# One recorded list of 2,598 steps sets the order of all five engines of a transformer-block kernel

## The chip, the cores and the metric

The kernel runs on one core of a Trainium2 chip. A core has five engines with a queue of instructions each: TensorE (PE, matrix products), VectorE (DVE), ScalarE (ACT), GpSimd (POOL) and SyncE (SP, which here only starts DMA transfers). The metric is the device time of one execution in microseconds (us), lower being better. Times come from the hardware: a median of several runs, and one profiled execution that leaves a trace of every instruction.

## The reference

One decoder layer on 512 tokens of width 1024, in float32, cut to what matters:

```python
h = x
h = h + 0.5 * swiglu(rmsnorm(h, ffn1_norm), ffn1_w_gate, ffn1_w_up, ffn1_w_down)      # width 2816
proj = rmsnorm(h, mix_norm) @ w_in
u, v, z, xbc, dt_raw = split(proj)
ya = chunked_spatial_gating(gelu(u), gelu(v), ln_g, ln_b, w_s, b_s)    # chunks of 128 tokens, causal
ya = rmsnorm(ya, gm_out_norm)
yb = mamba2_mixer(z, xbc, dt_raw, ...)     # convolution of 4 taps, 16 heads of 64, state 128, chunks of 128
h = h + concat([ya, yb]) @ w_out
h = h + 0.5 * swiglu(rmsnorm(h, ffn2_norm), ffn2_w_gate, ffn2_w_up, ffn2_w_down)
gate = sigmoid(rmsnorm(h, ple_norm) @ ple_w_gate + ple_b_gate)
h = h + gate * (p @ ple_w_proj)
return rmsnorm(h, final_norm)
```

## The kernel before

**Tiling.** Activations lie feature-major: `h` is eight tiles of 128 features x 512 tokens. Weights come in blocks of 128 x 1024 (512 KB) through the three buffers of `raw` and the like. Every block is split into two parts that the fast matmul format holds exactly: ScalarE casts the high part (`whi`, lines 185 and 421), VectorE subtracts it and leaves the low part (`wlo`, lines 186 and 422). A product then is three passes (lines 215 to 217, or 598 in the feed-forward blocks): high by high, low by high, high by low. Eight row blocks by three passes are 24 matmuls. The feed-forward blocks save products by a scheme in which seven sums of blocks are multiplied in place of eight; some of its sums are made by DMAs that GpSimd issues and that add while they load (lines 613, 616, 650).

**Stages.** (1) The embedding product `p @ ple_w_proj` in two halves (`embedding`, line 843), put into DRAM; (2) the first feed-forward block; (3) the mixer: the `w_in` products, convolution (959), step sizes and running sums, chunk states (1072; GpSimd's multiply at 1069, TensorE's products at 1076), two heads at a time the attention-like part (`decayed` 1095, `ssd` 1115), gating (`gated` 1138), the spatial gating (`mix` 1279); (4) `w_out` and the second feed-forward block; (5) the gate with the embedding (`gate` 1380), in the last three feature tiles by token halves (`gate_half` 1424), the final norm's sums (`factors` 1434) and the output tiles (`rows_out` 1445).

**Norms.** The mean square of a token is needed over features, which lie across partitions: ScalarE squares, VectorE or GpSimd adds up (267), TensorE multiplies by ones (276), VectorE finds the reciprocal root in small Newton steps (233 to 238), and a product with a diagonal spreads it to all partitions (`sm` at 306, kept as `rall` at 312). Products begin on unnormed data, and the factor is put in afterwards.

**What sets the order.** In stages (1), (2) and (4), `run` (line 348) issues steps by hand on PE, ACT, DVE and SP: loads 6 steps ahead, splits two ahead, what follows a product behind the next one. GpSimd is not in that order. The mixer and stage (5) are written as plain code, and the framework's scheduler orders them. A tile gets its buffer where the code asks for it. Of the eight PSUM banks three are for `mm`, two for `acc`, three for `sm`, each group in turn.

Of the kernel before, what the change touches and what calls it, by code (L numbers as in the profile page):

```python
# [42 lines left out]
AHEAD = 5  # L43
WARM = 10
BY_HALF = 3
LOADS = 6
# [3 lines left out]
    "nv": 2, "ny": 2, "nt": 2, "bnst": 2, "rlast": 2,  # L50
    "F": 1, "xfa": 2, "xfb": 2, "x": 16, "xs": 8, "u": 8, "emb": 8, "raw0": 1, "embt": 1, "rawb": 3,
# [30 lines left out]

@with_exitstack
def layer_kernel(ctx: ExitStack, tc: tile.TileContext, a: dict, out: bass.AP):
    nc = tc.nc
    PSUM = bass.MemoryType.PSUM
    base = ctx.enter_context(tc.tile_pool(name="sb", bufs=1))

    region = {"left": None, "right": None}
    names = {}  # L90
    count = [0]

    def pad(pool, name):
# [12 lines left out]
    def open_region(side, name):
        close_region(side)
        names[side] = name
        region[side] = tc.alloc_tile_pool(name=name, bufs=1, side=side, reuse_waits="tile")
        if side == "left":  # L110
            pad(region[side], name)

    psum = ctx.enter_context(tc.tile_pool(name="ps", bufs=1, space=PSUM))
    dram = ctx.enter_context(tc.tile_pool(name="dr", bufs=1, space=bass.MemoryType.DRAM))

    def sb(tag, shape=(P, T), dt=F32):
        count[0] += 1
        pool = region[REGION[tag]] if tag in REGION else base
        return pool.tile(list(shape), dt, tag=tag, bufs=BUFS.get(tag, 1), name=f"{tag}_{count[0]}")
# [4 lines left out]
    def bank(tag, n):  # L124
        count[0] += 1
        return psum.tile([P, T], F32, tag=tag, bufs=n, name=f"{tag}_{count[0]}")

    turns = {"mm": 0, "rawb": 0}

    def mm_ps():  # L130

        turns["mm"] += 1
        return bank("acc", 2) if turns["mm"] % 5 in (2, 4) else bank("mm", 3)

    def sm_ps():
        return bank("sm", 3)
# [25 lines left out]
    nc.scalar.copy(vec_warm, ones[:, 0:1])  # L162

    upper = sb("upper", (P, P))
    nc.gpsimd.affine_select(
        out=upper, in_=ones, pattern=[[1, P]], compare_op=ALU.is_ge, fill=0.0, base=0,
        channel_multiplier=-1,
    )
# [81 lines left out]
    class Norm:  # L250
# [18 lines left out]
        def sums(self):  # L269
# [4 lines left out]
            ps = sm_ps()  # L274
# [40 lines left out]
        @classmethod  # L315
        def on_all(cls, tok):
# [31 lines left out]
    def run(steps, opened=None):  # L348
# [8 lines left out]

        for i in range(LOADS):
            do(i, "load")
        for i in range(-3, n + 2):  # L360
# [7 lines left out]
            if i == opened:  # L368
                open_region("right", "ffn2_right")
                for k in held:  # L370
                    do(k, "load")
            late = 0 <= i - 1 < n and not steps[i - 1].urgent
            if 0 <= i - 2 < n and len(steps[i - 2].after) > 1:
                steps[i - 2].after[1]()
            for what in ("split", "after") if late else ("after", "split"):
# [460 lines left out]
    emb_dram = dram.tile([P, ND, T], F32, name="emb_dram", tag="emb_dram")  # L836
# [6 lines left out]
    def embedding(q):  # L843
# [46 lines left out]
    pad(base, "sb")  # L890
    x_ffn1, x_mix = [], []

    norm = Norm(nc.vector)
    steps, mix_norm = swiglu(
        "ffn1", x_ffn1, norm, lambda: open_region("left", "mix_left"),
# [11 lines left out]
    def squares(*ds):  # L907
        for d in ds:
            norm.add(h[d])
# [6 lines left out]
    for k, i in ((4, 3), (6, 2), (9, 4), (10, 1)):  # L916
# [7 lines left out]
    with tc.manual_schedule(engines=ORDERED):  # L924
        run(steps)
    norm = mix_norm
    open_region("right", "mix_right")


    x = x_mix  # L930
    w_in = a["w_in"]

    def project(unit, w=None):
        w = w or weights(w_in[unit], D)
        ps = mm_ps()
        accumulate(ps, w, 0, x)
        return ps
# [3 lines left out]
    w_dt = Unit(w_in[0], D)  # L941
    w_dt.load(0, D)
    nc.scalar.copy(w_dt.hi, w_dt.raw)
    both = w_dt.hi.rearrange("p (k m) -> p k m", k=ND)
    nc.vector.tensor_tensor(
        both[:, :, HEADS : 2 * HEADS],
        w_dt.raw.rearrange("p (k m) -> p k m", k=ND)[:, :, :HEADS],
        both[:, :, :HEADS].bitcast(F32), ALU.subtract,
    )
    ps = mm_ps()  # L950
    for n, k in enumerate(D_ORDER):
        for i in range(2):
            nc.tensor.matmul(
                ps, both[:, k, :], x[k][i], start=n + i == 0, stop=n + i == ND
            )
    dt_raw = tmp()
    nc.vector.tensor_copy(dt_raw[: 2 * HEADS], ps[: 2 * HEADS])

    def conv(ps, i, tag):
        raw = sb("convin", (P, T + 3))  # L960
        nc.vector.memset(raw[:, 0:3], 0.0)
        nc.vector.tensor_tensor(raw[:, 3:], ps, r, ALU.mult)
        o = sb(tag)
        nc.scalar.activation(
            o, raw[:, 0:T], AF.Identity, scale=col("conv_w", 4 * i), bias=col("conv_b", i)
        )
        for j in range(1, 4):
            nc.vector.scalar_tensor_tensor(
                o, raw[:, j : j + T], col("conv_w", 4 * i + j), o, ALU.mult, ALU.add
            )  # L970
        nc.scalar.activation(o, o, AF.Silu)
        return o
# [4 lines left out]
    early = [project(1)]  # L977
    rtok = norm.per_token(D)
    early.append(project(2))
    r = norm.on_all(rtok)  # L980
    bc = [conv(ps, 8 + i, "ya") for i, ps in enumerate(early)]
    dt_ps = sm_ps()
    for c in range(NC):
        nc.tensor.transpose(
            dt_ps[:, 2 * c * HEADS : 2 * (c + 1) * HEADS],
            dt_raw[: 2 * HEADS, c * P : (c + 1) * P], ident[: 2 * HEADS, : 2 * HEADS],
        )
    dtb = vec[:, _COL["dt_bias"] : _COL["dt_bias"] + HEADS]
    neg_a = sb("nega", (P, HEADS))
    nc.scalar.activation(neg_a, vec[:, _COL["a_log"] : _COL["a_log"] + HEADS], AF.Exp)  # L990
    nc.vector.tensor_scalar(neg_a, neg_a, -1.0, None, ALU.mult)
# [566 lines left out]
```

## Time and profile before

| | us |
|---|---|
| median of three runs | 1110.29 |
| lowest and highest of them | 1108.97, 1111.76 |
| span of the profiled execution | 1109.7 |
| TensorE busy in it | 1085.0 (98%) |
| VectorE | 781.7 (70%) |
| ScalarE | 513.8 (46%) |
| GpSimd | 132.0 (12%) |

The trace is read in this order: the page's busy times, then stretches of the span (busy time of each engine, the granted TensorE clock as a share of 2.4 GHz, the DMA engines' busy share), then what TensorE waited for, then timelines of single places. A busy TensorE is not TensorE at its peak, since matmuls overlap and their ends are modelled.

### The profile page before, as it was taken

How to read it: one execution, taken by the hardware profiler on the slowest of the kernel's cores; microseconds unless marked ns; L12 is line 12 of the kernel's file. 1: busy time of each engine (PE TensorE's matmuls, PEld its weight loads, DVE VectorE, ACT ScalarE, POOL GpSimd, SP SyncE). 2: the span in 40 equal slices, each digit the busy share in tenths (PEclk: the TensorE clock that was granted, in tenths of full speed). 3: DMA queues.
4: the chain of work that ended last, by engine and by line, in shares of the span. 5: the costliest groups of instructions: out<-in, count | busy, mean ns of one | idle time of the engine just before them, and what ended most of it. 6: DMA issues, size and time to landing. Idle time of an engine off the chain costs nothing.

```text
span 1109.7 us, 16404 instructions
## 1 busy us (share of the span) xinstructions
PE 1085.0 (98%) x6631; PEld 954.1 (86%) x6631; DVE 781.7 (70%) x1071; ACT 513.8 (46%) x709; POOL 132.0 (12%) x124
## 2 busy tenths in 40 slices
PE   9889999999999999999999999999999999999997
PEld 6779999999998787777888888889999999999887
DVE  5887776766667688576776664868767767667766
ACT  6545444444345374656443343544444443434554
POOL 2000000000001201244200000000000000000311
PEclk9999999999999999999999999999999999999998
DMA  9667757566631323234523233477677666643412
GB/s 353 201 164 202 198 153 190 163 188 155 184 95 57 96 79 107 95 112 133 160 78 96 76 95 114 146 175 194 188 190 189 177 185 174 163 123 110 138 54 76
DMA packets 49036, 161.66 MB, mean 146 GB/s; under 512 B 5568, under 2 KB 5824, under 8 KB 48960
## 3 DMA queue, kind: packets, MB, share of 16 engines
q1 hardware_dynamic: 34128, 117.46, 31.0%
q0 software_dynamic: 9232, 33.56, 16.7%
q10 hardware_dynamic: 5600, 9.60, 2.8%
q8 instruction: 52, 0.85, 0.3%
q14 instruction: 24, 0.20, 0.1%
HBM read 156.33 MB, written 4.26 MB: 145 GB/s over the span
## 4 chain that ended last, share of the span: by engine, by line
PE 83%; DVE 9%; ACT 4%; issue 2%; POOL 1%; DMA 1%; SPq 0%; DVEq 0%; ACTq 0%; POOLq 0%
PE mm L598 18%; PE acc L598 14%; PE sm L216 8%; PE sm L217 8%; PE sm L215 7%; PE mm L217 5%; PE mm L215 5%; PE mm L216 5%; PE acc L215 3%; PE acc L217 3%; PE acc L216 3%; DVE wlo L186 1%; ACT whi L421 1%; DVE wlo L422 1%; PE sm L1282 1%
## 5 line engine op out<-in xcount | busy, mean ns | idle before, releaser
L598 PE MATMUL mm<-xfb,whi 128*128 128x256 f32 x960 | 166.3, 276 | 0.5 <-ACT whi L421 0.5
L422 DVE TENSOR_TENSOR wlo<-raw,whi 128x1024 fp32r<-128x1024 f32 x93 | 113.9, 1225 | 54.5 <-ACT whi L421 53.0
L598 PEld LDWEIGHTS mm<-xfb,whi 128*128 128x128 f32 x960 | 145.9, 188 | 2.3 <-ACT whi L421 0.7
L598 PE MATMUL mm<-xfb,wlo 128*128 128x256 f32 x480 | 132.8, 277 | 0.8 <-DVE wlo L422 0.8
L421 ACT CAST whi<-raw 128x1024 fp32r<-128x1024 f32 x93 | 97.3, 1046 | 77.7 <-issue 39.5
L217 PE MATMUL sm<-ghi,wlox 128*128 128x512 f32 x296 | 116.3, 393 | 0.0
L216 PE MATMUL sm<-glo,whix 128*128 128x512 f32 x296 | 115.9, 391 | 0.0
L215 PE MATMUL sm<-ghi,whix 128*128 128x512 f32 x296 | 115.3, 389 | 0.0
L598 PE MATMUL acc<-xfb,whi 128*128 128x256 f32 x640 | 111.2, 276 | 0.8 <-DVE g L730 0.8
L598 PEld LDWEIGHTS acc<-xfb,whi 128*128 128x128 f32 x640 | 97.8, 188 | 2.9 <-issue 1.4
L598 PE MATMUL acc<-xfb,wlo 128*128 128x256 f32 x320 | 88.7, 277 | 2.6 <-DVE wlo L422 2.6
L598 PEld LDWEIGHTS mm<-xfb,wlo 128*128 128x128 f32 x480 | 90.1, 188 | 1.0 <-DVE wlo L422 1.0
L422 DVE TENSOR_TENSOR wlox<-rawd,whix 128x1024 fp32r<-128x1024 f32 (+1 forms) x40 | 45.7, 1142 | 57.8 <-ACT whix L421 57.8
L422 DVE TENSOR_TENSOR wlo<-rawb,whi 128x1024 fp32r<-128x1024 f32 x52 | 63.6, 1223 | 21.3 <-ACT whi L421 21.3
L736 ACT ACTIVATE g<-g 128x512 f32<-128x512 f32 x40 | 25.3, 632 | 110.8 <-DVE g L735 110.8
L185 ACT CAST whi<-raw 128x1024 fp32r<-128x1024 f32 x44 | 45.8, 1043 | 61.3 <-PE mm L216 22.6
L613 POOL DMA_DIRECT2D raw<-in_ffn_gu x20 | 17.6, 882 | 462.8 <-DVE xfb L486 163.6
L790 DVE SCALAR_TENSOR_TENSOR h<-sm,h 128x512 f32<-128x512 f32 x96 | 63.5, 684 | 10.9 <-PE sm L217 10.2
L186 DVE TENSOR_TENSOR wlo<-raw,whi 128x1024 fp32r<-128x1024 f32 x44 | 57.4, 1305 | 18.5 <-ACT whi L185 13.3
L217 PE MATMUL mm<-x,wlo 128*128 128x512 f32 x160 | 64.6, 404 | 4.2 <-DVE wlo L186 4.2
L421 ACT CAST whi<-rawb 128x1024 fp32r<-128x1024 f32 x52 | 54.2, 1042 | 26.4 <-DVE rawb L608 19.7
L217 PEld LDWEIGHTS sm<-ghi,wlox 128*128 128x128 f32 x296 | 55.5, 188 | 11.7
(392 smaller groups left out, 2620.7 us busy)
## 6 DMA issues: line engine op xcount, KB each, us to landing
raw<-in_ffn_gu SPq DMA_DIRECT2D x56, 512.0 KB, 5.7
rawd<-in_ffn_down SPq DMA_DIRECT2D x40, 512.0 KB, 4.0
rawb<-in_ffn_gu SPq DMA_DIRECT2D x32, 512.0 KB, 5.1
raw<-in_ffn_gu POOLq DMA_DIRECT2D x30, 512.0 KB, 5.4
raw<-in_w_in SPq DMA_DIRECT2D x29, 512.0 KB, 3.6
s<-in_ffn_gu SPq DMA_DIRECT2D x20, 512.0 KB, 7.2
s<-in_ffn_gu POOLq DMA_DIRECT2D x20, 512.0 KB, 8.2
raw<-in_w_out SPq DMA_DIRECT2D x16, 512.0 KB, 3.5
```

The source lines that it names most:

```text
L185: nc.scalar.copy(self.hi[:, c], self.raw[:, c])
L186: nc.vector.tensor_tensor(self.lo[:, c], self.raw[:, c], self.hi[:, c].bitcast(F32), ALU.subtract)
L215: nc.tensor.matmul(ps, whi, xhi, start=first, stop=False)
L216: nc.tensor.matmul(ps, whi, xlo, start=False, stop=False)
L217: nc.tensor.matmul(ps, wlo, xhi, start=False, stop=last)
L421: nc.scalar.copy(self.hi[:, :n], raw[:, :n])
L422: nc.vector.tensor_tensor(self.lo[:, :n], raw[:, :n], self.hi[:, :n].bitcast(F32), ALU.subtract)
L598: nc.tensor.matmul(o, wt[:, c], xt, start=fresh and p == m == n == 0, stop=last and n == 2, skip_group_check=True,)
L613: nc.gpsimd.dma_start(w21.raw, self.src[0], accum_op=ALU.add)
L736: nc.scalar.activation(t, t, AF.Silu)
L790: nc.vector.scalar_tensor_tensor(h[d], ps[d], 0.5, h[d], ALU.mult, ALU.add)
L1282: nc.tensor.matmul(chunk(ps, c), chunk(v[c][i // 4], i % 4), chunk(ws[i // 4], i % 4), start=True, stop=True,)
```

## The change

The code of the kernel now runs against a recorder: every operation is noted with its operands, and a tile is a `Spot` that has no place yet. What `run` and the mixer's parts write is a list of operations, cut into 2,598 units (matmuls in a row into one bank are one unit; all else is a unit by itself). Then `ORDER`, a table of all unit numbers, is gone through once, and each unit is issued for its engine, GpSimd's too. A tile takes the slot that has been free longest when its first operation is issued, and gives it back when its last one is issued. PSUM is eight banks of one kind (`b_...`). All instructions therefore have one line, 1943, in the new kernel.

```diff
+    def issue(i):
+        engine, what, args, kw = ops[i]
+        for t in spots[i]:
+            if t.real is None:
+                t.home.take(t)
+        getattr(getattr(real, engine), what)(...)
+        for t in spots[i]:
+            t.left -= 1
+            if t.left == 0:
+                t.home.back(t)
...
+ORDER = (
+    "6 1 5 0 7 9-10 2 13 11-12 3 20 14 21 18 16 24 77 15 19 25 17 26 41 27 29 42 40 39 37-38 28 30 32 8 "
...
+    with tc.manual_schedule(engines=ENGINES):
+        for u in order:
+            for i in units[u]:
+                issue(i)
...
-ORDERED = {
-    mybir.EngineType.PE, mybir.EngineType.Activation, mybir.EngineType.DVE, mybir.EngineType.SP
-}
+ENGINES = {
+    mybir.EngineType.PE, mybir.EngineType.Activation, mybir.EngineType.DVE, mybir.EngineType.Pool,
+    mybir.EngineType.SP,
+}
-AHEAD = 5
+AHEAD = 6
-LOADS = 6
+LOADS = 3
-    "nv": 2, "ny": 2, "nt": 2, "bnst": 2, "rlast": 2,
+    "nv": 2, "ny": 2, "nt": 2, "bnst": 4, "rlast": 2,
-    ... "u": 8, ...
+    ... "u": 9, ...
```

The mixer's code is cut into parts that can stand at any place of the list. Its arithmetic, the number and shapes of TensorE's matmuls and the bytes of the weights stay. ScalarE has six table loads more (21 for 15), VectorE one small copy more.

**Head, VectorE.** Before, around the running sums (`ssum`) of the first norm; `xfb` are expanded input halves, `wlo` weight splits:

```order
L542 TENSOR_TENSOR xfb_109<-ghi_291,xfb_109 128x512
L542 TENSOR_TENSOR xfb_111<-glo_293,xfb_111 128x512
L267 TENSOR_TENSOR ssum_299<-ssum_299,tmp_301 128x512
L267 TENSOR_TENSOR ssum_299<-ssum_299,tmp_304 128x512
L267 TENSOR_TENSOR ssum_299<-ssum_299,tmp_307 128x512
L422 TENSOR_TENSOR wlo_342<-rawb_134,whi_341 128x1024
L267 TENSOR_TENSOR ssum_299<-ssum_299,tmp_345 128x512
L267 TENSOR_TENSOR ssum_299<-ssum_299,tmp_348 128x512
L267 TENSOR_TENSOR ssum_299<-ssum_299,tmp_351 128x512
L267 TENSOR_TENSOR ssum_299<-ssum_299,tmp_354 128x512
L422 TENSOR_TENSOR wlo_382<-rawb_162,whi_381 128x1024
```

After, the running sums behind the first expanded input half (`xfa`):

```order
L1943 TENSOR_TENSOR wlo_106<-raw_100,whi_103 128x1024
L1943 TENSOR_TENSOR xfa_170<-ghi_208,xfa_170 128x2x512
L1943 TENSOR_TENSOR ssum_108<-ssum_108,tmp_90 128x512
L1943 TENSOR_TENSOR ssum_108<-ssum_108,tmp_89 128x512
L1943 TENSOR_TENSOR wlo_107<-raw_101,whi_256 128x1024
L1943 TENSOR_SCALAR glo_263<-h_97,vec_63 128x512
L1943 TENSOR_TENSOR wlo_265<-raw_90_173,whi_104 128x1024
L1943 TENSOR_TENSOR ssum_108<-ssum_108,tmp_258 128x512
L1943 TENSOR_SCALAR glo_268<-h_95,vec_63 128x512
L1943 TENSOR_TENSOR xfb_171<-glo_263,xfb_171 128x2x512
L1943 TENSOR_TENSOR ssum_108<-ssum_108,tmp_330 128x512
L1943 TENSOR_TENSOR glo_338<-glo_268,ghi_208 128x512
```

The sums moved from two rows of three and four, behind the second input half, to single places between splits and expansions, from the first half on.

On TensorE, before, all eight banks of the embedding product stand ahead of the first gate products; after, four embedding banks (`b_81` to `b_84`), then the gate products `b_85` and `b_86` over the first two input halves, then the other four embedding banks (`b_87` on).

**Mixer, VectorE.** Before, up to the weight split that ends at 466.96 us of the trace (`wlo_4588`); `xs`, `u` and `tmp` belong to head pairs, `yb` to chunk states:

```order
L1065 TENSOR_TENSOR yb_4513<-sm_4508,dt_3753 128x512
L186 TENSOR_TENSOR wlo_4499<-raw_4497,whi_4498 128x1024
L1131 SCALAR_TENSOR_TENSOR xs_3985<-xs_3985,vec_70,acc_4536 128x512
L1132 TENSOR_TENSOR u_4440<-u_4440,sm_4537 128x384
L1106 TENSOR_TENSOR u_4443<-u_4443,ya_4009 128x512
L1141 SCALAR_TENSOR_TENSOR tmp_4552<-mm_4472,rall_3725 128x512
L1081 TENSOR_TENSOR yb_4594<-yb_4505,etot_3946 128x512
L1106 TENSOR_TENSOR u_4445<-u_4445,ya_4009 128x512
L1082 TENSOR_TENSOR yb_4594<-yb_4594,sm_4592 128x512
L1065 TENSOR_TENSOR yb_4602<-sm_4597,dt_3753 128x512
L1143 SCALAR_TENSOR_TENSOR tmp_4552<-tmp_4553,tmp_4552 128x512
L186 TENSOR_TENSOR wlo_4588<-raw_4586,whi_4587 128x1024
```

After, a place with the same kind of steps:

```order
L1943 TENSOR_TENSOR wlo_4658<-raw_4625,whi_4633 128x1024
L1943 TENSOR_TENSOR ya_3644<-ya_3644,b_4574 128x384
L1943 SCALAR_TENSOR_TENSOR xs_3497<-xs_3497,vec_63,b_4614 128x512
L1943 TENSOR_TENSOR u_3508<-u_3508,ya_3648 128x512
L1943 TENSOR_TENSOR u_3511<-u_3511,ya_3648 128x512
L1943 SCALAR_TENSOR_TENSOR tmp_4629<-tmp_4643,tmp_4629 128x512
L1943 BN_STATS bnst_132<-ya_4562 128x6
L1943 TENSOR_TENSOR wlo_4666<-raw_4623,whi_4650 128x1024
L1943 TENSOR_TENSOR yb_3663<-b_4609,dt_121 128x512
L1943 TENSOR_TENSOR wlo_4669<-raw_4627,whi_4647 128x1024
L1943 SCALAR_TENSOR_TENSOR xs_3499<-xs_3499,vec_63,b_4704 128x512
L1943 SCALAR_TENSOR_TENSOR tmp_4755<-b_4713,rall_120 128x512
```

Splits moved together (`wlo_4666`, `wlo_4669`), and steps of different head pairs lie between those that need one another.

**End, ScalarE.** Before, from the last casts ahead of the spread factor `rall` on; `tmp` are sigmoids of the gate (`L1384`):

```order
L185 CAST whi_9895<-raw_9894 128x1024
L312 COPY rall_9793<-sm_9791 128x512
L1384 ACT_TABLE_LOAD
L1384 ACTIVATE tmp_9795<-tmp_9795,vec_70 128x512
L185 CAST whi_9934<-raw_9933 128x1024
L1389 ACTIVATE tmp_9800<-h_99 128x512
L1397 ACTIVATE h_99<-h_99,vec_70 128x512
L1384 ACTIVATE tmp_9804<-tmp_9804,vec_70 128x512
```

After:

```order
L1943 ACTIVATE tmp_9814<-h_94 128x512
L1943 COPY rall_9902<-b_9875 128x512
L1943 CAST whi_9904<-raw_9826 128x1024
L1943 CAST whi_9906<-raw_9824 128x1024
L1943 CAST whi_9908<-raw_9822 128x1024
L1943 ACT_TABLE_LOAD
L1943 ACTIVATE tmp_9914<-tmp_9914,vec_63 128x512
L1943 ACTIVATE tmp_9916<-tmp_9916,vec_63 128x512
```

All three last weight casts moved behind the factor and ahead of the table load and the first sigmoid.

**End, VectorE.** Before, around the last product (`sm_10140`); `rlast_10125` and `rlast_10210` are the final norm's factors of the two token halves, `o` output tiles:

```order
L238 SCALAR_TENSOR_TENSOR rlast_10125<-nt_10128,ny_10127 128x2
L1383 TENSOR_TENSOR tmp_10165<-sm_10140,rall_9793 128x256
L1455 TENSOR_SCALAR o_10186<-acc_10181,rlast_10125 128x512
L1385 TENSOR_TENSOR tmp_10165<-tmp_10165,emb_9704 128x256
L1455 TENSOR_SCALAR o_10202<-acc_10197,rlast_10125 128x512
L1386 TENSOR_TENSOR h_106<-h_106,tmp_10165 128x256
L1391 TENSOR_TENSOR tmp_10170<-h_106 128x256
L1399 TENSOR_SCALAR h_106<-h_106,vec_70 128x256
L243 TENSOR_SCALAR nv_10211<-sm_10205 128x2
```

After, around the last product (`b_10065`); the halves' factors are `rlast_138` and `rlast_139`, both found further down:

```order
L1943 TENSOR_TENSOR tmp_10139<-b_10065,rall_9902 128x256
L1943 TENSOR_TENSOR tmp_10144<-b_9965,rall_9902 128x256
L1943 TENSOR_TENSOR tmp_10146<-h_95 128x256
L1943 TENSOR_TENSOR tmp_10139<-tmp_10139,emb_9640 128x256
L1943 TENSOR_SCALAR h_95<-h_95,vec_63 128x256
L1943 TENSOR_TENSOR h_98<-h_98,tmp_10139 128x256
L1943 TENSOR_SCALAR nv_10166<-b_10153 128x2
L1943 TENSOR_SCALAR ny_10168<-nv_10166 128x2
L1943 TENSOR_TENSOR nt_10170<-ny_10168 128x2
```

The first half's factor and outputs moved behind the last product.

## Rows read from the trace of the kernel before

**Rows 1.** Busy time of each engine, the page: us (share), instructions.
```profile
PE 1085.0 (98%) x6631; PEld 954.1 (86%) x6631; DVE 781.7 (70%) x1071; ACT 513.8 (46%) x709; POOL 132.0 (12%) x124
```

**Rows 2.** Stretches: length, busy us per engine, PE clock, DMA share, GB/s.
```profile
0.00:30.00 30.00, 27.51 (x103) 20.87 (x104) 18.01 (x27) 18.75 (x28) 6.08 (x14) 1.00 0.95 347
30.00:60.00 30.00, 25.88 (x161) 21.97 (x159) 24.86 (x43) 16.43 (x24) 2.62 (x3) 1.00 0.66 179
...
90.00:360.00 270.00, 270.00 (x1900) 250.35 (x1899) 188.58 (x215) 116.62 (x142) 22.82 (x25) 1.00 0.58 159
...
450.00:480.00 30.00, 26.26 (x138) 20.01 (x137) 17.15 (x23) 17.64 (x41) 10.90 (x8) 0.94 0.31 96
```

**Rows 3.** TensorE's waits, 18.7 to 90 us: total us, times, longest.
```profile
PE acc L598 <- DVE wlo L422: 2.2, 2, 1.9
...
PE mm L215 <- ACT embt L881: 0.5, 1, 0.5
```

**Rows 4.** Timeline of TensorE at the sums: start, us, [idle before].
```profile
35.85 0.39 PE L216 MATMUL sm<-xfb,whi 128*128 128x512 f32 x1
36.08 0.40 PE L217 MATMUL sm<-xfb,wlo 128*128 128x512 f32 x1
37.48 0.72 PE L276 MATMUL sm<-ones,ssum 128*128 128x1 f32 x5 [1.00 <-DVE ssum L267]
```

**Rows 5.** Timeline of VectorE, same place.
```profile
31.01 2.29 DVE L267 TENSOR_TENSOR ssum<-ssum,tmp 128x512 f32<-128x512 f32 x3 [0.36 <-ACT tmp L266]
33.21 1.22 DVE L422 TENSOR_TENSOR wlo<-rawb,whi 128x1024 fp32r<-128x1024 f32 x1
34.35 3.08 DVE L267 TENSOR_TENSOR ssum<-ssum,tmp 128x512 f32<-128x512 f32 x4
```

**Rows 6.** TensorE's waits, 360 to 580 us (mixer).
```profile
PE mm L217 <- DVE wlo L186: 4.2, 3, 1.9
PE sm L1076 <- POOL u L1069: 2.1, 2, 1.5
```

**Rows 7.** Stretches right behind two stops in the mixer.
```profile
468.00:471.50 3.50, 3.50 (x10) 2.77 (x10) 2.29 (x3) 2.48 (x7) 1.30 (x1) 0.54 0.69 225
...
509.00:512.50 3.50, 3.50 (x10) 2.76 (x9) 1.79 (x2) 2.45 (x6) 0.55 (x1) 0.53 0.86 239
```

**Rows 8.** Timeline of all engines at the first of them.
```profile
465.11 1.85 DVE L186 TENSOR_TENSOR wlo<-raw,whi 128x1024 fp32r<-128x1024 f32 x1
465.83 2.00 POOL L1133 TENSOR_TENSOR xs<-xs,u 128x384 f32<-128x384 f32 x1
...
467.01 0.50 PE L217 MATMUL mm<-x,wlo 128*128 128x512 f32 x1 [1.95 <-DVE wlo L186]
```

**Rows 9.** GpSimd's state products: count, min/median/max ns.
```profile
L1069 POOL TENSOR_TENSOR u<-yb,toend x6: 1058/1709/2098, 425.4 to 477.5; 128x512 f32<-128x512 f32 x6
```

**Rows 10.** Timeline of ScalarE at a table load.
```profile
45.81 1.28 ACT L703 ACT_TABLE_LOAD   x1
47.10 1.15 ACT L703 ACTIVATE g<-g 128x512 f32<-128x512 f32 x2
```

**Rows 11.** Timeline of ScalarE at a load of running-sum rows.
```profile
454.65 1.57 ACT L1102 ACTIVATE u<-u,acs 128x128 f32<-128x128 f32 x5 [1.47 <-DMA u<-cs_dram]
```

**Rows 12.** Timeline of all engines, end of the program.
```profile
1094.80 0.15 DVE L233 TENSOR_SCALAR nv<-sm 128x2 f32<-128x2 f32 x1
...
1097.09 0.28 PE L217 MATMUL sm<-x,wlo 128*128 128x256 f32 x1
...
1098.28 0.42 DVE L1383 TENSOR_TENSOR tmp<-sm,rall 128x256 f32<-128x256 f32 x1
...
1101.50 0.38 PE L1440 MATMUL sm<-ones,tmp 128*128 128x1 f32 x2 [0.68 <-DVE tmp L1391]
...
1102.37 0.16 DVE L243 TENSOR_SCALAR nv<-sm 128x2 f32<-128x2 f32 x1 [0.53 <-PE sm L1440]
...
1103.66 1.41 DVE L1455 TENSOR_SCALAR o<-mm,rlast 128x512 f32<-128x512 f32 x2
```

More of the change, by code (lines that the diff above doesn't have):

```diff
@@ new lines, in _spots, with _units @@
+def _spots(op):
+    _, what, args, kw = op
+    operands = list(args) + [v for k, v in kw.items()]
+    seen = []
+    for x in operands:
+        if isinstance(x, Later) and x.spot not in seen:
+            seen.append(x.spot)
+    return seen
+def _units(ops):
+    units, last = [], None
+    for i, op in enumerate(ops):
+        key = None
+        if op[0] == "tensor":
+            key = op[2][0].spot
+        if key is not None and key is last:
+            units[-1].append(i)
+        else:
+            units.append([i])
+        last = key
+    return units
@@ L346, in __init__, with run @@
             self.rest = None
-    def run(steps, opened=None):
+    def run(steps, opened=None, works=None):
         n = len(steps)
@@ L359, in run, with extra @@
             do(i, "load")
+        def extra(i, late):
+            for key, fn in sorted((works or {}).get(i, ()), key=lambda t: t[0]):
+                if (key >= 0.2) == late:
+                    fn()
         for i in range(-3, n + 2):
@@ L920, in layer_kernel, with at @@
     also(steps[4], "split", store_embedding)
-    ORDERED = {
-        mybir.EngineType.PE, mybir.EngineType.Activation, mybir.EngineType.DVE, mybir.EngineType.SP
-    }
[L924 to L927, printed above, removed]
+    works = {}
+    ffn1_steps, mixer = steps, []
+    def at(k, fn):
+        whole = int(k)
+        works.setdefault(len(ffn1_steps) + whole, []).append((round(k - whole, 6), fn))
     x = x_mix
     w_in = a["w_in"]
[L933 to L937, printed above, removed]
@@ L956, in layer_kernel @@
[L956 to L972, printed above, removed]
+    got = {}
@@ new lines, in layer_kernel, with projection, product, dt_step @@
+    small = lambda tag: sb(tag, (P, HEADS * NC))
+    def projection(unit, where):
+        w = Parts()
+        def product():
+            got[unit] = where()
+            accumulate(got[unit], (w.hi, w.lo), 0, x)
+        return Step(product, lambda: w.load(w_in[unit]), None, w.split)
+    def dt_step():
+        w = Parts()
+        def split():
+            w.hi = sb("whi", (P, 1024), F32R)
+            nc.scalar.copy(w.hi, w.raw)
+            both = w.hi.rearrange("p (k m) -> p k m", k=ND)
+            nc.vector.tensor_tensor(
+                both[:, :, HEADS : 2 * HEADS],
+                w.raw.rearrange("p (k m) -> p k m", k=ND)[:, :, :HEADS],
+                both[:, :, :HEADS].bitcast(F32), ALU.subtract,
+            )
+        def product(first=0, end=6):
+            both = w.hi.rearrange("p (k m) -> p k m", k=ND)
+            if first == 0:
+                got["dt"] = bank_at(0, "dt")
+            for n in range(first, end):
+                for i in range(2):
+                    nc.tensor.matmul(
+                        got["dt"], both[:, D_ORDER[n], :], x[D_ORDER[n]][i],
+                        start=n + i == 0, stop=n + i == ND,
+                    )
+        at(0.9, lambda: product(6, ND))
+        return Step(product, lambda: w.load(w_in[0]), None, split)
@@ new lines, in first_step, with product, dt_out @@
+    def first_step():
+        w = Parts()
+        def product(first=6, end=ND):
+            if first == 0:
+                got[1] = bank_at(1, "bc")
+            for n in range(first, end):
+                d = D_ORDER[n]
+                c = slice(d * P, (d + 1) * P)
+                passes(got[1], w.hi[:, c], w.lo[:, c], *x[d], n == 0, n == ND - 1)
+        at(0.01, lambda: product(0, 6))
+        return Step(product, lambda: w.load(w_in[1]), None, w.split)
+    def dt_out():
+        got["dt_raw"] = tmp()
+        nc.vector.tensor_copy(got["dt_raw"][: 2 * HEADS], got["dt"][: 2 * HEADS])
@@ L1362, in layer_kernel @@
     also(steps[8], "split", lambda: XForms.t1(x_ffn2))
-    with tc.manual_schedule(engines=ORDERED):
-        run(out_steps + steps, opened=len(out_steps) - 1)
+    run(
+        ffn1_steps + mixer + out_steps + steps,
+        opened=len(ffn1_steps) + len(mixer) + len(out_steps) - 1, works=works,
+    )
     norm = ple_norm
```

738 lines of the change are left out of this document (481 added, 257 removed), and 116 rows, old and new, of the table ORDER.

## The prediction

> **What bounds the kernel now.** I read the page's busy times first: TensorE works 1085.0 of 1109.7 us [rows 1], so a new order alone can take at most the 24.7 us in which it idles, and what its busy time hides. The table of stretches says where that is [rows 2]. From 90 to 360 us, most of the first feed-forward block, it is busy without a gap, and the second block does the same work; nothing is to be won there. The idle time lies in the first 90 us, in the mixer, and behind the last product.
>
> *Head.* The list of TensorE's waits between 18.7 and 90 us has eight lines, from 2.2 to 0.5 us, 7.1 us in all at nine stops [rows 3]. A stop costs more than its idle time: matmuls begin 0.23 us apart but a row is 0.39 us long, so a stopped engine drains for another 0.16 us that counts as busy [rows 4]. That makes 7.1 + 9 x 0.16 = 8.5 us. At 37.48 the norm's sums wait 1.0 us for VectorE's last running sum, because VectorE begins its seven additions only at 31.01 [rows 4, 5].
>
> *Mixer.* The waits between 360 and 580 us (five lines, the first two stand in the rows) are 4.2 us for three weight splits, 2.1 us for the products that GpSimd makes for the chunk states, 0.8 us for the convolution input, and two of 0.3 and 0.2 us: 7.6 us idle at eight stops, with their drains 8.9 us [rows 6]. And where TensorE had stood 1.95 us, its granted clock in the next 3.5 us was 0.54 of 2.4 GHz (about its 1.2 GHz level), a second time 0.53 [rows 7, 8]: 3.5 x 0.46 x 2 = 3.2 us. Together 12.1 us. The trace says why the split came late: VectorE reaches it at 465.11, behind a step that needs a product TensorE has just made, and then it takes 1.85 us, where one with GpSimd idle takes 1.22 [rows 5, 8].
>
> *Tail.* The last product ends at 1097.37, the last output tile 7.7 us later at 1105.07 [rows 12]. The program ends at 1109.7.
>
> **The change, part by part.** TensorE does the same matmuls in both kernels; so all comes from stops. The steady stretches have none, so they stay.
>
> *Head, gains.* The order now puts the first two gate products ahead of the second half of the embedding product, and the running sums one by one between VectorE's other work. Take the sums that waited at 37.48. In the new order TensorE, without the earlier stops, reaches them at about 36.4 us, where it also was before (37.48 less the wait). VectorE has, behind the second expanded input half (needed by TensorE at about 14.7 us, counted in matmuls of 0.23 us), 24 instructions up to the last running sum: 7 over 1,024 columns, 1.14 us from start to start, and 17 shorter ones of at most 0.76 us (2.29 for three) [rows 5], 20.9 us at most. So the sum is there at 35.6, 0.8 us early. The same count at the later stops (weight splits, first hidden values) finds 0.3 to 3 us to spare and no stop up to 72 us. I take the whole 8.5 us. The thin places are the second expanded half (0.3 us spare) and a combined weight block whose accumulating DMA lands some 3 us before its use, where the first 30 us have the DMA engines 0.95 busy [rows 2]. If those fail, 4 us of the 8.5 stay away; if the trace has drained more than I count, 10 can go.
>
> *Mixer, gains.* The mixer is now one list. On VectorE splits stand next to each other and steps of different head pairs between those that need one another; on TensorE whole products of 24 matmuls (24 x 0.23 = 5.5 us) lie between the head pairs' eight-matmul products, which is time for VectorE. Counting TensorE's work between the matmul that releases a run of VectorE or ScalarE work and the one that needs it, against the run's length plus 0.3 us, the old order is short by 0.5 to 2.2 us in four places between 440 and 485 us, which are its stops; the new order is short nowhere, with 0.3 to 0.95 us to spare in the tightest. One stop I expect to stay: two of GpSimd's state products are now wanted one matmul apart, with 3.9 us of TensorE work behind their source, and they take 0.7 (VectorE) + 2 x 1.7 (GpSimd) + 0.6 us (handing over) = 4.7, so 0.8 us [rows 9]. GpSimd still lies on VectorE's instructions, which will open one or two of the tight places: 2 us more. Of 12.1 us I take 12.1 - 0.8 - 2.3 = 9; at worst 2, at best 12.
>
> *Mixer, cost.* ScalarE gets six more table loads, since Gelu and Exp now alternate. One was 1.28 us, and the ACTIVATE behind it began 0.01 us after it [rows 10]. Six are 7.7 us on an engine that is busy 17.64 of 30 us from 450 to 480 [rows 2]; covered by the 12 us it has free there I cost them at nothing, and if the cover fails a load is one late cast: with all six uncovered the sum is 1104 instead of 1096. The Trainium skill (ScalarE: Activation LUTs, What ACT_TABLE_LOAD costs) states 1283 ns for the load and about 1380 ns of drain with it, 2.66 us a switch. The load agrees; the drain does not show in this trace, neither ahead of the load nor behind it. By the page six switches would be 16 us, and the sum with all of them uncovered 1112.
>
> *Tail, loss.* Before, the first token half's sums were taken ahead of the last product, and its factor and four output tiles came while the second half still computed. Now both halves' sums follow the last product. On ScalarE the cast of the last weights waits for a buffer, and the table load and the sigmoids stand behind it, so that VectorE arrives at the last product with no lead. Worked out from its end with before's rows [rows 12]: VectorE reads it 0.9 us later (as before), three 256-column steps 1.2, TensorE's sums 0.9 (1101.50 to 1102.37), the first factor 3.5 (1094.80 to 1098.28, with two other steps in between, now three), the first output 0.7, a table load 1.28, the root and the last steps of the second factor 1.1 (of the 1.29 between 1102.37 and 1103.66), two outputs 1.4: 11.0 us instead of 7.7. The sums' matmuls no longer stand ahead of the last product, which gives 0.9 us back; eight output DMAs in a row instead of four and four take 0.2. That is 2.6; with a lag of VectorE, which I put at 0.4 us, 3 us slower, and between 1 and 5.
>
> *Sum:* 1109.7 - 8.5 - 9 + 3 = 1095.2 us. The median of the runs shown is 0.6 above the profiled execution, so 1095.8, rounded 1096. The best ends give 1109.7 - 10 - 12 + 1 + 0.6 = 1089, the worst of this case 1109.7 - 4.5 - 2 + 4 + 0.6 = 1108.
>
> **Rivals.** *Slower: ScalarE's queue in the mixer.* It holds the weight casts, the exponentials, six more table loads, and the loads of the running-sum rows, for which its exponentials already wait up to 1.47 us [rows 11]. In a fixed list everything behind such a wait is late, the next cast too, then its split, then TensorE, and a stop of 2 us brings half clock for another 1.6 us [rows 7, 8]: 3.6 us each. Some eleven weight blocks pass between 440 and 520 us. The old stops are gone (-12.1), head and tail give -5.5; from six such stops on (+21.6) the kernel is slower than before by 4 us, with seven it stands at 1110.3 - 17.6 + 25.2 = 1118. Against it: the row loads are issued long before, and the row counted above has spare time there.
>
> *No change: the DMAs pace the head, and the mixer's stops only move.* A TensorE that is 8 us ahead at 60 us asks for the same bytes earlier, and the first 30 us already have 0.95 of the DMA engines [rows 2]. If the head gives only 2 us, the mixer 3, and the tail costs 3, it is 1108. For it speaks that accumulating loads take longest there; against it that from 30 us on the share is 0.66.
>
> *That the list is not followed* can be set aside: the build's order on every engine shows it.
>
> **How the numbers follow.** A measurement of this kernel tells 0.3% (3.3 us) from no change. The forecast (TensorE without the head's stops and with few of the mixer's) gets 0.82, no change 0.09, slower 0.09. The forecast's own ends, 1089 to 1107, hold nearly all of its 0.82. To have 8 in 10 the range goes 2 us below, for drains that I may have counted short, and 1 above: 1087 to 1108. So faster 0.82, same 0.09, slower 0.09.
>
> **What would show it.** In the changed kernel's trace: TensorE's waits between 18 and 90 us below 2 us, and the sums at about 36.5; waits in the mixer below 4 us and no stretch with the clock near 0.5; still a wait for GpSimd's state products; a busy TensorE in both feed-forward blocks as before; last product near 1079 and some 11 us from its end to the last output tile. It is wrong if weight splits or casts in the mixer wait again by 2 us, if the head's landings end TensorE's waits, or if the tail is longer than 13 us.

## The result, and the profile after

Side by side on one chip, 20 runs each, the changed kernel takes 1113.99 us (1112.37 to 1116.24) and the kernel before 1111.88 us (1108.97 to 1113.63): a ratio of 1.0024, with a 95% interval of 1.0017 to 1.0031. It is 2 us slower, within the 0.3% that I called no change; 1096 was forecast, and the range ended at 1108. The profiled execution has a span of 1113.4 us, against 1109.7 before.

Three views show that the stops behind the first 18.7 us went much as forecast. The page's busy times, against [rows 1], then the table of stretches, against [rows 2] (length; busy us of TensorE, its weight loads, VectorE, ScalarE, GpSimd; granted clock of TensorE, DMA share, GB/s):

```profile
PE 1099.0 (99%) x6631; PEld 967.6 (87%) x6631; DVE 765.0 (69%) x1072; ACT 520.2 (47%) x715; POOL 127.5 (11%) x124
```

```profile
30.00:60.00 30.00, 30.00 (x203) 27.40 (x202) 27.20 (x45) 17.01 (x25) 4.78 (x7) 1.00 0.78 206
90.00:360.00 270.00, 270.00 (x1832) 249.23 (x1831) 181.99 (x213) 116.34 (x140) 19.73 (x24) 1.00 0.56 154
...
450.00:480.00 30.00, 29.71 (x151) 23.25 (x150) 22.08 (x32) 26.86 (x54) 4.26 (x4) 1.00 0.50 151
```

From 30 to 60 us TensorE no longer idles at all (25.88 of 30 us busy before), and from 450 to 480 it is busy for 29.71 instead of 26.26 us, at full clock. Its list of waits for 18.7 to 90 us is empty, where [rows 3] begins a list of 7.1 us; ahead of 18.7 us it has become longer, 3.5 us instead of 1.9, with two new waits for ScalarE's `ghi`. For the mixer, 360 to 580 us, the list is now (total us, times, longest), against [rows 6]:

```profile
PE b L1943 <- DVE wlo L1943: 1.0, 2, 0.7
PE b L1943 <- ACT x L1943: 0.4, 1, 0.4
PE b L1943 <- DVE x L1943: 0.3, 1, 0.3
```

That is 1.7 us instead of 7.6. And yet TensorE's busy time is 14 us higher, with the same 6,631 matmuls. The timeline of TensorE in the first feed-forward block tells why. It shows runs of 72 matmuls of 256 columns in a row without a stop, first and last row of each. The kernel before:

```profile
202.98 0.39 PE L598 MATMUL acc<-xfb,whi 128*128 128x256 f32 x2
...
211.03 0.28 PE L598 MATMUL acc<-xfa,wlo 128*128 128x256 f32 x1
```

The changed kernel:

```profile
200.47 0.39 PE L1943 MATMUL b<-xfb,whi 128*128 128x256 f32 x2
...
208.83 0.28 PE L1943 MATMUL b<-xfa,wlo 128*128 128x256 f32 x1
```

From the first start to the last it is 8.05 us before and 8.36 after; over 71 distances that is 113.4 and 117.7 ns. Nothing waits in either. Taken over all rows of a kind (start to start, where no stop lies between), a 256-column product of `xfb` went from 113.4 to 117.7 ns and a 512-column product of `x` from 227.7 to 232.6. About 3,350 matmuls of the first kind at 4.2 ns are 14 us, all in the feed-forward blocks, where I had said that nothing changes; some 800 of the second at 5 ns are 4 us. That is 18 us (the expectations below took 640 of the second kind, and so 17 us). Other products (of `ya` and `yb`) kept their pace of 227 ns.

One difference of the built programs I had not looked at: where in SBUF, the memory that holds the kernel's tiles, each of them lies. `bnst` has four buffers instead of two, two times 64 bytes, and so the regions behind it, with these tiles, begin 128 bytes further. Taken mod 512, `xfa` and `xfb` moved from 320 to 448, and `x`, `xs` and `u` from 384 to 0. The weight tiles `whi` and `wlo` (384) and `ya` and `yb` (384) stayed.

The end of the program, timeline of all engines in the changed kernel (start, length, operation, [idle before <- ended by]), against [rows 12]:

```profile
1094.32 0.28 PE L1943 MATMUL b<-x,wlo 128*128 128x256 f32 x1
...
1096.52 0.75 DVE L1943 TENSOR_TENSOR tmp<-b,rall 128x256 f32<-128x256 f32 x2
...
1099.00 3.65 PE L1943 MATMUL b<-ident,h 128*128 128x128 f32 x16
...
1102.45 0.43 PE L1943 MATMUL b<-ones,ssum 128*128 128x1 f32 x2
...
1104.19 0.16 DVE L1943 TENSOR_SCALAR nv<-b 128x2 f32<-128x2 f32 x1 [1.72 <-PE b L1943]
...
1107.35 1.41 DVE L1943 TENSOR_SCALAR o<-b,rlast 128x512 f32<-128x512 f32 x2 [0.76 <-PE b L1943]
```

The last product ends at 1094.60 and the last output tile at 1108.76: 14.2 us, where it was 7.7 before and 11.0 were forecast. VectorE reads the last product 1.9 us after its end. TensorE, busy for only 0.76 of the 3.00 us from 1095 us on, works at a granted clock of 0.50 behind that, its 1.2 GHz level:

```profile
1095.00:1098.00 3.00, 0.76 (x5) 0.67 (x5) 2.93 (x9) 2.71 (x6) 0.86 (x2) 0.86 0.03 5
1098.00:1102.50 4.50, 4.50 (x23) 4.37 (x23) 3.63 (x16) 2.23 (x5) 0.73 (x1) 0.50 0.01 2
```

### The profile page after: what moved, and what is told of

Its sections match the earlier page's. It is cut to its first block, busy times and chain, and to the rows that moved or that the text cites. A ratio compares the mean times of both kernels' runs of the same rounds, so it can differ in the third digit from the quotient of the medians.

```text
span 1113.4 us, 16384 instructions
## 1 busy us (share of the span) xinstructions
PE 1099.0 (99%) x6631; PEld 967.6 (87%) x6631; DVE 765.0 (69%) x1072; ACT 520.2 (47%) x715; POOL 127.5 (11%) x124
## 3 DMA queue, kind: packets, MB, share of 16 engines
q0 software_dynamic: 9232, 33.56, 16.3%
## 4 chain that ended last, share of the span: by engine, by line
PE 92%; DVE 5%; DMA 1%; ACT 1%; issue 1%; POOL 0%; ACTq 0%; SPq 0%; POOLq 0%
PE b L1943 92%; DVE tmp L1943 1%; DVE wlo L1943 1%; DVE xs L1943 1%; DMA g<-in_p 1%; DVE u L1943 0%; DVE x L1943 0%; DVE h L1943 0%; POOL ssum L1943 0%; DVE ya L1943 0%; DMA cs_dram<-csrow 0%; DVE yb L1943 0%; ACT tmp L1943 0%; DVE convin L1943 0%; ACT whi L1943 0%
## 5 line engine op out<-in xcount | busy, mean ns | idle before, releaser
L1943 PE MATMUL b<-xfb,whi 128*128 128x256 f32 (+1 forms) x1664 | 305.8, 284 | 0.0
L1943 PEld LDWEIGHTS b<-xfb,whi 128*128 128x128 f32 x1664 | 259.2, 188 | 7.0 <-issue 1.0
L1943 PE MATMUL b<-xfb,wlo 128*128 128x256 f32 (+1 forms) x832 | 236.3, 284 | 0.0
L1943 DVE TENSOR_TENSOR wlo<-raw,whi 128x1024 fp32r<-128x1024 f32 (+1 forms) x139 | 173.8, 1254 | 66.3 <-ACT whi L1943 66.3
L1943 ACT CAST whi<-raw 128x1024 fp32r<-128x1024 f32 (+1 forms) x140 | 145.1, 1040 | 147.5 <-PE b L1943 107.4
L1943 PE MATMUL b<-x,whi 128*128 128x512 f32 (+1 forms) x640 | 189.3, 382 | 0.7 <-ACT x L1943 0.4
L1943 PEld LDWEIGHTS b<-xfb,wlo 128*128 128x128 f32 x832 | 156.2, 188 | 1.4
L1943 PE MATMUL b<-xfa,whi 128*128 128x256 f32 (+1 forms) x704 | 134.4, 289 | 0.0
L1943 PE MATMUL b<-x,wlo 128*128 128x512 f32 (+1 forms) x312 | 117.9, 378 | 0.3 <-DVE wlo L1943 0.3
L1943 PE MATMUL b<-ghi,whix 128*128 128x512 f32 x296 | 116.6, 394 | 0.0
```

The lines of the kernel that those rows point to most:

```text
L1943: getattr(getattr(real, engine), what)(*(real_of(x) for x in args), **{k: real_of(x) for k, x in kw.items()})
```

## Experiments: is it the addresses or the order?

**The changed kernel at the old addresses.** Theory A: where the moving tile (a matmul's operand that is not its weight) lies sets the pace of the matmuls. Theory B: the new order itself does, by what stands beside a matmul or which bank it writes. `PAD` holds bytes that each region begins with, so addresses can be moved without touching an instruction. The first run moves `xfa`, `xfb`, `x`, `xs` and `u` back, the second `xfa` and `xfb` alone.

```diff
-PAD = {..., "ffn_left": 96, "mix_left": 160, "ple_left": 160, ...}
+PAD = {..., "ffn_left": 480, "mix_left": 32, "ple_left": 32, ...}     # e1_after_pads
+PAD = {..., "ffn_left": 480, "mix_left": 160, "ple_left": 160, ...}   # e1_after_ffnpad
```

> The changed kernel with one line edited: the pads that open the three left regions of SBUF, ffn_left 96 to 480, mix_left 160 to 32, ple_left 160 to 32 bytes. In the changed kernel xfa, xfb, x, xs and u lie 128 bytes further (mod 512) than in the kernel before, because more small tiles lie below them; with these pads their addresses mod 512 are those of the kernel before again (320 for xfa and xfb, 384 for x, xs and u). Order, waits and instructions are the changed kernel's. Theory A, the address of the moving operand sets the pace of the matmuls: 256-column products in the feed-forward blocks fall from 117.6 ns start to start to 113.4, 512-column products of x from 232.7 to 227.7, and the time falls by about 3,350 x 4.2 ns + 640 x 5 ns = 17 us, from 1114 to 1097. Theory B, the new order itself (which instruction stands beside a matmul, which PSUM bank it writes) sets the pace: spacing stays at 117.6 and 232.7 and the time at 1114, within 3 us.

> The changed kernel with only ffn_left 96 to 480, so that xfa and xfb alone stand at the residue of the kernel before (320 mod 512), while x, xs and u stay at 0. Theory A: 256-column products back at 113.4 ns, those of x still at 232.7; 3,350 x 4.2 ns = 14 us of the 17, so 1114 - 14 = 1100. Theory B: no change of either, 1114.

With all of them back the time is 1096.1 us (1095.1 to 1099.5), 0.988 of the kernel before (0.986 to 0.990; before 1110.7 on this chip). With `xfa` and `xfb` alone it is 1101.1 (ratio 0.991, 0.990 to 0.993). The same run of 72 matmuls in the first of them, timeline of TensorE:

```profile
163.13 0.39 PE L1943 MATMUL b<-xfb,whi 128*128 128x256 f32 x2
...
171.18 0.28 PE L1943 MATMUL b<-xfa,wlo 128*128 128x256 f32 x1
```

It takes 8.05 us again, as in the kernel before. In the costliest groups (busy us, mean ns of one | idle before) the mean length of a row goes up and down with the distance. The changed kernel:

```profile
L1943 PE MATMUL b<-xfb,whi 128*128 128x256 f32 (+1 forms) x1664 | 305.8, 284 | 0.0
L1943 PE MATMUL b<-x,whi 128*128 128x512 f32 (+1 forms) x640 | 189.3, 382 | 0.7 <-ACT x L1943 0.4 <-DVE x L1943 0.3
L1943 PE MATMUL b<-whi,x 128*128 128x512 f32 x128 | 42.7, 401 | 0.0
```

With all of them moved back:

```profile
L1943 PE MATMUL b<-xfb,whi 128*128 128x256 f32 (+1 forms) x1664 | 296.6, 281 | 0.0
L1943 PE MATMUL b<-x,whi 128*128 128x512 f32 (+1 forms) x640 | 186.8, 378 | 0.7 <-ACT x L1943 0.5 <-DVE x L1943 0.3
L1943 PE MATMUL b<-whi,x 128*128 128x512 f32 x128 | 42.1, 396 | 0.0
```

With `xfa` and `xfb` alone moved back:

```profile
L1943 PE MATMUL b<-xfb,whi 128*128 128x256 f32 (+1 forms) x1664 | 296.5, 281 | 0.0
L1943 PE MATMUL b<-x,whi 128*128 128x512 f32 (+1 forms) x640 | 189.3, 382 | 0.7 <-ACT x L1943 0.4 <-DVE x L1943 0.3
```

Each of these kinds of product changes when its own tile is moved and not otherwise: 281 for `xfb`, still 382 for `x` (378 with all moved back). Theory B, that the new order is what costs, falls.

**The kernel before at the new addresses.** The same from the other side: 128 bytes more in each of the three pads, and then the one number of the change that did it.

```diff
-PAD = {..., "ffn_left": 96, "mix_left": 160, "ple_left": 160, ...}
+PAD = {..., "ffn_left": 224, "mix_left": 288, "ple_left": 288, ...}   # e2_before_pads
-    ... "bnst": 2, ...
+    ... "bnst": 4, ...                                                # e2_before_bnst4
```

> The kernel before with 128 bytes more in each of the three left pads, so that xfa, xfb, x, xs and u stand at the residues of the changed kernel (448 and 0 mod 512) and nothing else differs. Theory A: 256-column products at 117.6 instead of 113.4 ns, those of x at 232.7 instead of 227.7, and the time up by 17 us, from 1111 to 1128. Theory B: spacing and time as in the kernel before, 1111.

> The kernel before with one number of the change alone: four buffers for bnst instead of two. That is the part of the change that shifts the left regions by 128 bytes, without the new order. Theory A: as with the pads, 117.6 and 232.7 ns and about 1128. Theory B: 1111, or a little less if the two more buffers free VectorE's statistics from a wait.

They take 1125.6 and 1126.1 us, both 1.014 of the kernel before (1.012 to 1.015), where 1128 was expected. In the second, 256-column products of `xfb` are 117.5 ns apart and 512-column ones of `x` 232.5. So two small buffers cost the kernel before 15 us, and the four times make a square:

| | old addresses | new addresses |
|---|---|---|
| order before | 1110.7 | 1125.6 |
| new list | 1096.1 | 1114.0 (before on that chip: 1111.9) |

The list alone gives 14.6 us, the addresses alone take 14.9; together they take 2, which is 1 to 2 us more than the sum.

## Experiments: what about the address?

**Other places.** Two good and two bad places say little of the rule. These kernels are the changed one with other pads, one run each (beside the kernel before at 1110.6 us for the three s, at 1112.3 us for t and w); the numbers in their names are the places of `xfa` and `xfb`, and of `x`, mod 512.

> The changed kernel with other pads: xfa and xfb at 64, x, xs and u at 128 bytes mod 512, which is 256 bytes from where the kernel before has them (320 and 384). If what counts is the address mod 256, both are as in the kernel before: 113.4 ns for 256-column products of xfb, 227.7 ns for 512-column products of x, and a time of 1097. If the period is 512 or longer, at least one of the two is at another value.

> The changed kernel with xfa and xfb at 384, x, xs and u at 320 mod 512, which swaps the two good places. If a place is good for whatever tile lies there (ya and yb are at 384 in both kernels and their pace did not change), both paces are as in the kernel before, 113.4 and 227.7 ns, and the time is 1097. If it is the distance to the weight tiles or the length of the row that counts, one of them is slow, 117.6 or 232.7.

> The changed kernel with xfa and xfb at 0, x, xs and u at 448 mod 512, the two bad places swapped. If a place is bad for whatever tile lies there, 117.6 and 232.7 ns as in the changed kernel and a time of 1114. If not, one of the two is fast.

> The changed kernel with xfa and xfb at 352, x at 416 mod 512, places between the measured ones: distances to the weight tiles of -32 (256-column products) and +32 (512-column products). Distance theory, between its measured neighbours: 256 columns between 113.4 (at -64) and 119.8 (at 0), 512 columns between 227.4 (at 0) and 229 (at +64), time between 1097 and 1120. A pace below 113 or 227 would be a better place than that of the kernel before.

> The changed kernel with xfa and xfb at 288, x at 352 mod 512, distances of -96 and -32. Distance theory, between its measured neighbours: 256 columns between 118.8 (at -128) and 113.4 (at -64), 512 columns between 233.2 (at -64) and 227.4 (at 0), time between 1097 and 1116.

**Other places for the weights.** Is it the moving tile's own place or its distance to the weight tile? Here `whi` and `wlo` go from 384 to 0 and all behind them stays, once with the restored pads (w1) and once with the changed kernel's own (w2).

```diff
             for tag, (shape, dt) in self.tags.items():
+                gap = {"whi": 128, "ssum": 384}.get(tag, 0) if self.name == "sb" else 0
+                if gap:
+                    pool.tile([P, gap // 4], F32, tag=f"gap_{tag}", name=name_of("gap"))
```

> The changed kernel with restored pads (xfa and xfb at 320, x at 384 mod 512) and the weight tiles whi and wlo moved by 128 bytes, from 384 to 0 mod 512; everything behind them is where it was. If the distance between the moving tile and the weight tile counts, mod 256, this is again the changed kernel's distance: 117.6 ns for xfb, 232.7 ns for x, and now also some 232.7 instead of 227 for ya and yb, time 1096 + 17 + 2 = 1115. If the place of the moving tile alone counts, nothing changes: 113.4, 227.4, 227, time 1097.

> The changed kernel with its own pads (xfa and xfb at 448, x at 0 mod 512) and whi and wlo moved by 128 bytes to 0 mod 512, so that the distances to xfa, xfb and x are those of the kernel before. Distance theory: 113.4 and 227.4 ns without the moving tiles being where they were, ya and yb at 232.7, time 1114 - 17 + 2 = 1099. Place theory: 117.6, 232.7, 227, time 1114.

Measured: mean ns from start to start, where no stop lies between, and the time ("col." are columns, `xf` is `xfa` and `xfb`). "Distance" is the place of the moving tile less that of the weight tile, mod 256, for `xf` and for `x`.

| kernel | distance `xf`, `x` | 256 col., `xfb` | 512 col., `xf` | 512 col., `x` | 256 col., `x` | us |
|---|---|---|---|---|---|---|
| before | -64, 0 | 113.4 | 233.3 | 227.7 | 119.9 | 1111 |
| changed | +64, -128 | 117.7 | 229.7 | 232.6 | 118.6 | 1114.0 |
| e1_after_pads | -64, 0 | 113.5 | 232.9 | 227.3 | 119.9 | 1096.1 |
| s1_64_128 | -64, 0 | 113.5 | 232.9 | 227.4 | 119.9 | 1097.6 |
| s2_384_320 | 0, -64 | 119.8 | 227.6 | 233.3 | 113.1 | 1120.3 |
| s3_0_448 | -128, +64 | 118.8 | 233.2 | 229.0 | 117.8 | 1115.1 |
| t1_352_416 | -32, +32 | 118.2 | 233.2 | 233.2 | 116.9 | 1117.1 |
| t2_288_352 | -96, -32 | 118.6 | 234.1 | 233.2 | 118.3 | 1118.3 |
| w1_weights | +64, -128 | 117.8 | 228.8 | 232.6 | 118.4 | 1115.6 |
| w2_weights | -64, 0 | 117.1 | 233.3 | 227.2 | 119.9 | 1111.6 |

Four things follow. A period of 256 bytes fits: 64 and 128 do what 320 and 384 do. It is not the tile: in s2 `xf` and `x` change places, and each takes over the other's pace at the same column count. It is the column count together with the place: a distance of 0 is best for 512 columns (227 ns) and worst for 256 (120), while -64 is best for 256 (113) and slow for 512 (233). So `xf`, read mostly in 256 columns, and `x`, read mostly in 512, want different places; the kernel before had both. And the expectation that places in between are in between was wrong: 256 columns at -32 and -96 and 512 columns at -32 and +32 are as slow as the bad places. The two kernels for it (t1, t2) are also the only ones with `xf` and `x` at no multiple of 64 bytes, so whether the distance or that makes them slow is open.

Beyond that, the distance theory held for the 512-column products of `x`, `xf`, `ya` and `yb`: every distance that was measured more than once gave the same pace within 1 ns. The products of `ghi` and `glo` with `whix` and `wlox`, at distance 0 in every kernel (all at 480), fit it less well: 228 to 230 ns on average, by kernel, where the others have 227. In w1 `x`, `ya` and `yb` lie where they lay in `e1_after_pads`, and only the weights moved; the costliest groups of w1:

```profile
L1946 PE MATMUL b<-xfb,whi 128*128 128x256 f32 (+1 forms) x1664 | 305.7, 284 | 0.0
L1946 PE MATMUL b<-x,whi 128*128 128x512 f32 (+1 forms) x640 | 189.2, 382 | 0.7 <-ACT x L1946 0.4 <-DVE x L1946 0.3
L1946 PE MATMUL b<-yb,whi 128*128 128x512 f32 x128 | 40.8, 400 | 0.0
L1946 PE MATMUL b<-whi,x 128*128 128x512 f32 x128 | 42.7, 401 | 0.0
```

`xfb` is at 284 and `x` at 382, the changed kernel's values, and `yb`, which had 396 in the changed kernel with either pads, now 400 (from start to start 232.3 instead of 227.5). The last row is the product in which `x` is the weight and `whi` moves: it too follows the distance (401 here and in the changed kernel, 396 with the restored pads).

For 256 columns the mean held in w1 (117.8 expected and found) and failed in w2: at distance -64, 117.1 ns instead of 113.4, so w2 takes 1111.6 us where 1099 was expected. Why it can fail shows when the matmuls are taken series by series, a series being 256-column products of `xf` in a row with no stop and no other product between. At distances of +64 and -64 there are two paces, 113.3 and 117.8 ns, and every series of 20 or more has, behind its first few matmuls, one of them to its end, in the kernel before too. With the addresses restored, where 113.3 is the rule, one series is (timeline of TensorE, its first and last `wlo` row, 45 distances):

```profile
719.06 0.28 PE L1943 MATMUL b<-xfb,wlo 128*128 128x256 f32 x1
...
724.36 0.28 PE L1943 MATMUL b<-xfb,wlo 128*128 128x256 f32 x1
```

That is 117.8 ns. In the changed kernel, where 117.8 is the rule, one series has 21 distances of 113.3 ns:

```profile
754.95 0.28 PE L1943 MATMUL b<-xfb,wlo 128*128 128x256 f32 x1
...
757.33 0.28 PE L1943 MATMUL b<-xfb,wlo 128*128 128x256 f32 x1
```

So the address does not fix the pace of these products; it goes with how often each of the two comes. Of about 3,300 matmuls in such series 3,160 are at 113.3 with the addresses restored, 23 in the changed kernel, 356 in w2 (as from 73.4 to 86.2 us), with no tile moved in between. What else decides, beside the distance, stays open. At the other distances tried (0, -32, -96, -128) no series is at 113.3.

## Experiment: the tail

With the addresses restored, the timeline of all engines has these last rows of a product and of an output tile:

```profile
1076.24 0.28 PE L1943 MATMUL b<-x,wlo 128*128 128x256 f32 x1
...
1088.14 0.69 ACT L1943 ACTIVATE o<-b,rlast 128x512 f32<-128x512 f32 x1 [0.25 <-PE b L1943]
```

That is 12.3 us from 1076.52 to 1088.83; before it was 7.7. The list has the norm's last squares behind two weight casts, and takes the gate products in an order in which neither token half is finished early. The last numbers of the list, 160 of them, were set anew.

```diff
-... 2433 2492 2449 2408 2410 2479 2468 2417-2418 2420 2469 2480 2506 2500 2503 2434-2445 2450 2470 2451 ...
-... 2517 2560 2532 2509 2525 2540 ... (products; last of the first token half: 2525)
+... 2433 2492 2408 2410 2479 2420 2417 2418 2503 2468 2480 2500 2434 2449 2435-2438 2469 ... 2450 2451 2470 ...
+... 2517 ... 2509 ... 2525 ... 2540 ... 2532 ... 2548 ... 2560 ... (2548: the first half's sums)
```

> The changed kernel with the pads that restore the old addresses, and with the last 180 numbers of its list set anew: the squares of the last norm ahead of two weight casts, its sums one product earlier, the gate products in the order first token half, second token half, and the first half's sums ahead of the last product, as in the kernel before. Theory: the list's tail costs, since the span from the end of the last product to the end of the program is 16.9 us in the changed kernel with restored pads and 12.3 in the kernel before; it should fall to 11 to 12.5 and the time by 4 to 6 us against the run with restored pads (1096.1), to about 1091. Rival: the tail is bounded by VectorE's and ScalarE's sum of work whatever the order, and the time stays at 1096, within 2 us.

It takes 1092.65 us (1092.3 to 1095.1), 0.984 of the kernel before (0.982 to 0.986): 3.5 us less than `e1_after_pads`, a little less than expected; the intervals of the two ratios to the kernel before don't overlap. Three things of the tail were changed at once, and what each gives is not shown. Its timeline of all engines from the last product on:

```profile
1079.62 0.28 PE L1943 MATMUL b<-x,wlo 128*128 128x256 f32 x1
...
1079.74 1.91 PE L1943 MATMUL b<-ident,h 128*128 128x128 f32 x16
...
1081.17 0.42 DVE L1943 TENSOR_TENSOR tmp<-b,rall 128x256 f32<-128x256 f32 x1
...
1084.10 0.54 PE L1943 MATMUL b<-ones,tmp 128*128 128x1 f32 x2
1084.50 3.42 PE L1943 MATMUL b<-ident,h 128*128 128x128 f32 x16
...
1087.96 0.75 DVE L1943 TENSOR_SCALAR o<-b,rlast 128x512 f32<-128x512 f32 x1 [0.73 <-PE b L1943]
```

From the last product's end to the last output tile it is 8.8 us instead of 12.3. The first 16 transposes now take 1.91 us, where the changed kernel's took 3.65: TensorE comes to them straight from the product, at a granted clock of 1.00. The second 16 still take 3.42, behind 4.5 us in which TensorE was busy for 2.90, with a granted clock of 0.57 from 1084.5 to 1088 us. This kernel takes less time than either of the two.

## Why the prediction was wrong, point by point

**The step that failed** is this one: "TensorE does the same matmuls in both kernels; so all comes from stops. The steady stretches have none, so they stay." Most of the same matmuls ran 4 to 5 ns further apart because two small buffers moved their operands. That is 18 us by the distances from start to start, and 16 to 18 us by the times (1.0024 against 0.9877 of the kernel before, or 1114.0 against 1096.1 us). The number was in the diff (`bnst`, 2 to 4), and I gave it no cost. None of the rivals had it either. The sign that I had named for these stretches, a TensorE that is busy as before, came true (270.00 of 270.00 us in both kernels) and could not show it.

**The list's own gain** was sized well: 1096 was forecast, and with the old addresses it is 1096.1. That the two meet so closely is luck: by the profiled executions (1109.7 and 1093.4 us) the list gives 16.3 us where 14.5 were forecast, more from head and mixer and less from the tail. By parts, with the end of the first block read from the last product of `ghi` with its weights; before, changed, and with restored pads:

```profile
364.31 0.39 PE L217 MATMUL sm<-ghi,wlo 128*128 128x512 f32 x1
```

```profile
362.73 0.39 PE L1943 MATMUL b<-ghi,wlo 128*128 128x512 f32 x1
```

```profile
354.84 0.39 PE L1943 MATMUL b<-ghi,wlo 128*128 128x512 f32 x1
```

- **Head**, forecast -8.5: -9.5 with the old addresses. In the changed kernel only 1.6 are left of it, the pace of the block having eaten most of the rest.
- **Mixer**, forecast -9, and -0.9 for the sums that no longer stand ahead of the last product: from 364.31 to the last product's end was 733.1 us, with the old addresses it is 721.7, so -11.4. The stop of 0.8 us at GpSimd's state products, which I expected to stay, is not there; no stretch of 30 us in the mixer has the granted clock below 1.00.
- **Table loads**, costed at nothing: no cast of ScalarE makes TensorE wait in the mixer, and the splits that do cost 1.0 us in all. The rival of ScalarE's queue did not come. Nor did the one of the DMAs: none of TensorE's waits in the first 90 us is put down to a landing, with a DMA share of 0.78 from 30 to 60 us.
- **Tail**, forecast +3.9 against the last product's end (3 with the 0.9): +4.6 with the old addresses, +6.5 in the changed kernel. The place was right, the size not, and the 14.2 us of the changed kernel are past the 13 that I had named as a sign of being wrong: VectorE's lag was 1.9 us behind the product and not 1.3, and I had not counted that TensorE, idle for most of 3 us, would do its sums and transposes at 1.2 GHz. The second half's sums take 1.7 us (1102.45 to 1104.19) instead of 0.9.
- **Figures that don't agree with each other**: the mixer's sum takes off 2.3 us where its text says 2, and the worst end is 1108 in the sum and 1107 in the chances. Neither changes the outcome.

## What to carry to other kernels

A stretch in which an engine is always busy is not a stretch that stays: compare the distance from start to start of its instructions in both traces before looking for stops. When a change alters the number or size of any tile, see which operands of matmuls move, and pad them back to their old place mod 256 bytes, so that order and layout are measured apart; here a gain of 14.6 us was hidden by 128 bytes. Choose the place by the column count of the matmuls that read the tile, and measure it, since neighbouring places are not in between, and a mean can hide two paces.

## What the runs showed that I had not expected

The pace of matmuls at full clock goes with the distance in bytes between the moving tile and the weight tile: 227 to 234 ns for 512 columns, and on average 113 to 120 for 256, without any wait. Since moving the weights alone changes the pace of products whose moving tile stayed (`yb`, 227.5 to 232.3), the pace depends on the place of both operands. The Trainium skill (TensorE: Matmul & The Clock Gate, Step-by-step: what each phase is for) says that the two have their own read ports, and that loading the next weights takes no SBUF bandwidth from the running matmul; taken as a promise that the weights' place costs the running matmul nothing, that differs from these runs by 2% for `yb`, and the runs decide. How the two meet is not shown by them, nor what puts a series of 256-column products at one or the other of its two paces.
